# An encoder trunk on one core: large tiles in one common set, B outputs as one run, another opening, grouped norm steps and a last product with the gate inside its weights

## The chip, the cores and the metric

The kernel runs on one core of a Trainium2 chip. The metric is the device time of one execution in microseconds (us); the kernel before has a median of 739.84 us over 3 runs (739.37 to 739.89). A difference of about 0.2% (1.5 us) is the least that such a measurement can tell from no change.

## What is computed

Two layers over x of 256 rows by 1024 columns. Each layer mixes tokens by two attention branches, A (8 query heads on 2 key heads, dense) and B (3 dilated groups of 4 heads, combined by their softmax denominators), gated and summed, and then channels by a squared-ReLU MLP. Both halves have an RMS norm with shift, scale and gate from a vector c.

```python
for l in range(2):
    sh1, sc1, gt1, sh2, sc2, gt2 = split(silu(c) @ w_ada[l] + b_ada[l], 6)
    h = rms(x, g_mix[l]) * (1 + sc1) + sh1
    parts = split(h @ w_in[l])                    # 1024 x 5120: A's q, k, v; B's 3 x (q, k, v); 2 gates
    y_a = attention(rope(rms(qa)), rope(rms(ka)), va) @ w_branch_a[l]
    y_b = dilated(rope(rms(qb)), rope(rms(kb)), vb) @ w_branch_b[l]
    x = x + gt1 * ((sigmoid(ga) * y_a + sigmoid(gb) * y_b) @ w_out[l])
    h2 = rms(x, g_mlp[l]) * (1 + sc2) + sh2
    x = x + gt2 * (square(relu(h2 @ w_ff1[l])) @ w_ff2[l])
```

## The kernel before

**Precision and weights.** Every float32 weight tile of 128 x 1024 (512 KB) is loaded from HBM into one of 7 buffers `wr`; ACT copies it to a rounded high part and DVE subtracts to get the low part (`split_next`). A product then takes three matmuls, high by high, low by high and high by low (`mm3`, `many`). So 512 columns of output cost TensorE (PE) three passes, and each weight tile costs ACT one and DVE one instruction of 1024 columns.

**The vector c.** 96 more tiles of 512 KB (`w_ada`) go through `wr` as well; DVE multiplies each by silu(c) and sums it along the row, in one instruction (`ada_tile`). Their place among the rest is written into the lists `seq0`, `seq1` (letter w), `ada_f0` and `ada_f1`.

**Order of the work.** The program text records operations. A planner (`Plan.issue`) then runs a list scheduler with a cost for each operation, due times, the number of buffers of each kind and pauses for clashes between DVE and GpSimd (POOL), and writes each engine's instructions out in the planned order; the chip keeps that order and waits where the plan was wrong. Letters in `seq0` and `seq1` set the order in which the mixer's parts are recorded: `c` is a chunk of 512 columns of q, k, v, `u` and `v` a half of a gate, `a` and `b` steps of the two attentions, `y` the product with w_branch_a. `OPEN` sets the first loads, the order of the first steps and the engine of each small operation of the opening; `shift` moves due times of single operations.

**Opening.** x comes in two halves, `x0` (with identity, biases and tables, 128 x 1552) and `x1` (128 x 1280); `a0` and `a1` are the first two tiles of w_ada (shift and scale of the first 128 columns of h), `wx` and `wy` the first tiles of w_in (chunks 0 and 1; 2 and 5). `step_x` norms and transposes a half of x, `step_a` makes shift and scale, `step_h` h's first 128 columns, `step_m` its product with wx or wy. One of the two, wy, is used plain in float32, without a split. From then on the loop over k = 1 to 7 does, for each k, two ada tiles, two weight tiles and 24 matmuls.

**Norm of q and k.** `qk_post` takes a chunk's sums from PSUM: ACT copies and squares, DVE sums the squares over each head (`rstd`), adds epsilon, POOL raises to the power -0.5, and DVE combines `t1` (sum by cosine table, read from PSUM) with `t2` (by sine table, POOL's in layer 0, DVE's in layer 1), multiplies by `rstd`, and PE transposes the result.

**Attention.** `att_a_soft` and `att_b_soft` (before: `att_b_pair`) take scores from PSUM, make probabilities `pr`, transpose them on PE, and ACT copies the transposes to SBUF (`keep_pt`, before: buffers of the small kind `s2k`). The products with the values have 64 output columns, two at a time side by side on PE. In B each of two pairs of heads has its own run of 12 such products.

**MLP.** `ff1` makes 512 hidden columns at a time; their squares are split into high and low (`split_hid`, before: `r2k`, 8 small buffers). The last product of layer 1 is cut so that the last output is 256 columns wide; then DVE multiplies by the gate (`gtb`), adds x, and a DMA writes out.

**Buffers.** `b8` is the common set of 8 KB tiles per partition (split weights, hT, tables, attention): 14 before. `s2k` has 7 tiles of 2 KB.

## Time and profile before

| what | value |
|---|---|
| median of 3 runs | 739.84 us |
| the profiled execution | 738.93 us |
| its span, first to last instruction | 737.1 us |
| granted TensorE clock, mean | 0.999 |
| PE busy | 728.7 us (99%) |
| DVE busy | 591.1 us (80%) |
| ACT busy | 469.9 us (64%) |
| POOL busy | 70.2 us (10%) |
| HBM | 178.73 MB read, 244 GB/s over the span |

Matmuls are pipelined, so the busy time of PE is not its work at the peak; what counts is where a matmul starts later than the one before it would allow. In rows of the timeline the columns are start (us from the span's start), length (us), engine, line, operation, what it writes and reads, its form (for PE rows by columns of the array, then the output), count, and in brackets the idle time before it and what ended it. All operations have line 655, at which the planner issues them, so rows are told apart by their tiles: `w` is a split weight, `wr` a raw one, `ps` a PSUM bank, `xin` holds x and the identity, `hT` the transposed and split h, `s2k` any small tile. A float32 matmul (a transpose, or scores) is recorded as more than one.

### The profile page before, as it was taken

The numbers are of one execution on the slowest core, as the hardware profiler recorded it, in microseconds if no ns is written. First come the engines' busy times: TensorE is split into PE (matmuls) and PEld (weight loads), VectorE is DVE, ScalarE is ACT, GpSimd is POOL, SyncE is SP. The second block draws the span as 40 slices with busy tenths as digits, with TensorE's granted clock in tenths as the row PEclk, the third lists the DMA queues.
The fourth block names the chain that finished last, engine by engine and source line by source line (L and its number), as shares of the span: only waits on it lengthen the run. The fifth ranks groups of instructions, "written<-read, shape, count | busy, mean of one in ns | idle before, by whom it ended". The sixth has DMA issues, their size and how long they took to land.

```text
span 737.1 us, 10423 instructions
## 1 busy us (share of the span) xinstructions
PE 728.7 (99%) x3750; PEld 601.1 (82%) x3750; DVE 591.1 (80%) x906; ACT 469.9 (64%) x784; POOL 70.2 (10%) x60
## 2 busy tenths in 40 slices
PE   8999999999999999999999999999999999999998
PEld 5887877788888888888887788877888888888887
DVE  6999999899899989575499977988878975675623
ACT  6569497975758666655366856698537866455530
POOL 0008730000000060000002211000000000000000
PEclk9999999999999999999999999999999999999999
DMA  9997578997499999776256555988546986686201
GB/s 352 409 409 241 158 241 268 337 334 258 144 351 380 392 340 321 260 243 198 70 167 229 183 175 161 369 293 315 193 142 192 371 279 191 223 275 191 77 1 57
DMA packets 50227, 180.47 MB, mean 245 GB/s; under 512 B 5600, under 2 KB 6016, under 8 KB 50176
## 3 DMA queue, kind: packets, MB, share of 16 engines
q1 hardware_dynamic: 50176, 179.82, 69.6%
q8 instruction: 29, 0.48, 0.3%
q14 instruction: 22, 0.18, 0.1%
HBM read 178.73 MB, written 1.06 MB: 244 GB/s over the span
## 4 chain that ended last, share of the span: by engine, by line
PE 94%; DVE 3%; ACT 1%; DMA 1%; POOL 1%; issue 0%; SPq 0%
PE ps L655 94%; DVE s2k L655 1%; DMA wr<-in_w_ada 1%; ACT s2k L655 1%; DVE rstd L655 1%; POOL rstd L655 0%; ACT pr L655 0%; SPq L655 0%; POOL s2k L655 0%; ACT hT L655 0%; DVE w20wx L655 0%; DVE w L655 0%; DVE shg L655 0%; DVE xT L655 0%; DVE tabs L655 0%
## 5 line engine op out<-in xcount | busy, mean ns | idle before, releaser
L655 DVE TENSOR_TENSOR w<-wr,w 128x1024 fp32r<-128x1024 f32 x234 | 284.5, 1238 | 55.6 <-ACT w L655 55.2
L655 ACT ACTIVATE w<-wr 128x1024 fp32r<-128x1024 f32 x234 | 242.3, 1059 | 82.7 <-PE ps L655 56.5
L655 PE MATMUL ps<-w,hT 128*128 128x512 f32 x1032 | 251.1, 396 | 0.1
L655 PEld LDWEIGHTS ps<-w,hT 128*128 128x128 f32 x1032 | 189.7, 188 | 41.9 <-issue 2.2
L655 PE MATMUL ps<-w,r2k 128*128 128x512 f32 (+1 forms) x792 | 178.8, 385 | 0.0
L655 PEld LDWEIGHTS ps<-w,r2k 128*128 128x128 f32 x792 | 144.5, 188 | 30.1
L655 PE MATMUL ps<-hT,w 128*128 128x512 f32 (+1 forms) x896 | 159.7, 338 | 0.0
L655 PEld LDWEIGHTS ps<-hT,w 128*128 128x128 f32 x896 | 138.1, 188 | 20.3
L655 DVE CUSTOM_DVE_ANT_0 s2k<-wr,c_act 128x1024 bf16<-128x1024 f32 x96 | 116.6, 1227 | 3.2 <-DMA wr<-in_w_ada 3.1
L655 ACT ACTIVATE s2k<-ps 128x512 f32<-128x512 f32 (+2 forms) x136 | 61.4, 483 | 77.1 <-PE ps L655 67.0
L655 PE MATMUL ps<-w,mT 128*128 128x512 f32 x192 | 45.6, 393 | 0.0
L655 ACT ACTIVATE s2k<-s2k 128x512 f32<-128x512 f32 (+1 forms) x62 | 38.5, 620 | 6.6 <-DVE s2k L655 5.8
L655 PEld LDWEIGHTS ps<-w,mT 128*128 128x128 f32 x192 | 35.6, 188 | 7.2
L655 POOL TENSOR_TENSOR rstd<-rstd,half 128x8 f32<-128x8 f32 (+1 forms) x20 | 34.5, 1738 | 68.9 <-DVE rstd L655 68.8
L655 ACT ACTIVATE pr<-pr,st 128x256 f32<-128x256 f32 (+1 forms) x64 | 36.1, 611 | 3.0 <-DVE st L655 3.0
L655 DVE TENSOR_TENSOR s2k<-ps,s2k 128x256 f32<-128x256 f32 x56 | 23.4, 420 | 16.8 <-ACT s2k L655 16.7
L655 POOL TENSOR_TENSOR ss<-ss,half 128x1 f32<-128x1 f32 x8 | 4.4, 556 | 296.2 <-DVE ss L655 296.2
L655 DVE TENSOR_TENSOR r2k<-s2k,r2k 128x512 fp32r<-128x512 f32 x28 | 20.1, 719 | 15.5 <-ACT r2k L655 15.2
L655 DVE TENSOR_TENSOR s2k<-ps,gtb 128x512 f32<-128x512 f32 (+1 forms) x18 | 11.8, 660 | 23.6 <-PE ps L655 23.4
L655 PEld LDWEIGHTS ps<-xin,s2k 128*128 128x128 f32 x180 | 21.2, 140 | 7.8 <-ACT pr L655 1.3
L655 PE MATMUL ps<-xin,s2k 128*128 128x128 f32 x180 | 26.4, 275 | 1.1 <-ACT pr L655 0.9
L655 ACT ACTIVATE s2k<-xin 128x512 bf16<-128x512 f32 x14 | 8.7, 623 | 26.4 <-DVE xin L655 26.1
(97 smaller groups left out, 512.0 us busy)
## 6 DMA issues: line engine op xcount, KB each, us to landing
wr<-in_w_ff SPq DMA_DIRECT2D x120, 512.0 KB, 5.0
wr<-in_w_ada SPq DMA_DIRECT2D x96, 512.0 KB, 5.2
wr<-in_w_gate SPq DMA_DIRECT2D x32, 512.0 KB, 4.5
wr<-in_w_qkv SPq DMA_DIRECT2D x24, 512.0 KB, 4.8
wr<-in_w_x SPq DMA_DIRECT2D x16, 512.0 KB, 5.9
wr<-in_w_out SPq DMA_DIRECT2D x16, 512.0 KB, 5.3
wr<-in_w_y SPq DMA_DIRECT2D x8, 512.0 KB, 6.5
wr<-in_w_ba SPq DMA_DIRECT2D x8, 512.0 KB, 6.3
```

Source lines behind the costliest of these rows:

```text
L655: getattr(self.real[o["e"]], o["op"])(*map(real, o["a"]), **{n: real(z) for n, z in o["k"].items()})
```

## The change

- The squares of the hidden columns (`hid`), B's transposed outputs (`ob`) and the attentions' transposed probabilities (`pt_home`) become tiles of the common set `b8`, now of 16; `r2k` and `ob` as kinds of their own are gone, `s2k` grows from 7 to 9.
- B's products with the values, 24 of a layer, are recorded as one run after the second pair's softmax (`att_b_out`).
- The opening loads x0, a0, a1, x1, wy, wx in place of x0, x1, a0, a1, wx, wy, does its steps in another order, and has other engines for seven of its small operations. The mask is loaded after the opening's weights and not before 62 us of the plan (in place of after k = 3).
- In `qk_post`, adding epsilon to `rstd` and the product `t1` are a group: DVE does them one right behind the other.
- At the end of layer 1, of the last 256-column products, those with the last two weight tiles use weights that DVE has multiplied by the gate, rounded and split beforehand (`gated`). They stand behind all others, in banks of their own, so that what is left after the last matmul is one addition.
- The lists `seq0`, `seq1`, `ada_f0`, `ada_f1`, `shift` and some constants of the planner's model (COLD, RATE, SOON, the cost of a copy from PSUM) have new values.

```diff
-  post0=(5, 2, 1, 0), s2k=7, r2k=8, ahead=1, last="k",
+  post0=(5, 2, 1, 0), s2k=9, ahead=1, last="k",
-  seq0="v u c3 w a w c4 v w w u a w b w w u w w w w w a a v w w v w w b w y w y w w w w v y y w w".split(),
-  seq1="w w a w c2 u c3 a u w w c4 v u c5 w w w w b b v v w w w a u w a w y w w w w w y w v y y w w w".split())
+  seq0="a v u c3 a w w w w w c4 v w u w w a w w u b v a w w w v y w w w w w b w w w y w w y y v w".split(),
+  seq1="a a w w a w w c2 u c3 a c5 u w w w w w w u c4 w v w b b v y v u v y w w y w w w w w w w y w w".split())
-NB8 = 14
+NB8 = 16
-    loads="x0 x1 a0 a1 wx wy",
-    steps="C T1 X0 A X1 H0 Wx H1 Mx0 Wy My0 T0 My1 Mx1",
+    loads="x0 a0 a1 x1 wy wx",
+    steps="T1 C Wy A X0 T0 H0 Wx X1 H1 Nx0 Lx0 My0 Mx1 My1",
...
-        dve.tensor_scalar(r, r, HD * EPS, None, op0=ALU.add)
+        with plan.together():
+            dve.tensor_scalar(r, r, HD * EPS, None, op0=ALU.add)
+            dve.tensor_tensor(v4(t1), v4(ps[:, :n]), bc(ct, HD), op=ALU.mult)
         pool.tensor_tensor(r, r, half[:, :nh], op=ALU.pow)
-        dve.tensor_tensor(v4(t1), v4(ps[:, :n]), bc(ct, HD), op=ALU.mult)
...
+    def pt_home(nm):
+        return tl("sbuf", [P, 4, 512], F32, "b8", NB8, f"pT{nm}")
...
         for hp in range(2):
-            att_b_pair(l, T, hp, ops)
+            zs.append(att_b_soft(l, T, hp))
             if hp == 1:
+                ops = pb(f"ob{l}")
+                with plan.together():
+                    for i in range(2):
+                        att_b_out(T, i, zs[i], ops)
                 finish_o(ops, T["ob"], slice(0, 2))
...
         def hid_tiles(j):
-            return [(r2k(f"hh{l}_{j}_{u}"), r2k(f"hl{l}_{j}_{u}")) for u in range(2)]
+            z = tl("sbuf", [P, 2, 2, 512], F32R, "b8", NB8, f"hid{l}_{j}")
+            return [(z[:, u, 0], z[:, u, 1]) for u in range(2)]
...
+        gated = tl("sbuf", [P, 2, 2, 512], F32R, "b8", NB8, "gated")
+        for q, (_, _, w) in enumerate(ws[6:]):
+            wg = s2k(f"wg{q}")
+            dve.tensor_tensor(wg, raw_of[w[0].tile.name][:, 512:1024], gtb[l, 1][:, 512:1024], op=ALU.mult)
+            act.activation(gated[:, q, 0], wg, AF.Copy)
+            dve.tensor_tensor(gated[:, q, 1], wg, f32(gated[:, q, 0]), op=ALU.subtract)
...
+        for c0 in halves:
+            cs = slice(c0, c0 + 256)
+            acc = pb(f"gated{c0}")[:, :256]
+            for q, (j, i, w) in enumerate(ws[6:]):
+                wh, wl = (gated[:, q, z, c0 - 512 : c0 - 256] for z in range(2))
+                mm3(acc, *last_rows(j, i), wh, wl, q == 0, q == 1)
+            dve.tensor_tensor(x[:, 1, cs], x[:, 1, cs], acc, op=ALU.add)
             sp.dma_start(out[1, :, cs], x[:, 1, cs])
```

Three places of the instructions as they stand. First, the loads on SP's queue from the start of the program; before:

```order
L655 DMA c_in<-in_c 128x136
L655 DMA xin<-in_x 128x1552
L655 DMA xin<-in_x 128x1280
L655 DMA wr_83<-in_w_ada 128x1024
L655 DMA wr_84<-in_w_ada 128x1024
L655 DMA wr_85<-in_w_x 128x1024
L655 DMA wr_86<-in_w_y 128x1024
L655 DMA wr_87<-in_w_ada 128x1024
```

and of the change:

```order
L666 DMA c_in<-in_c 128x136
L666 DMA xin<-in_x 128x1552
L666 DMA wr_83<-in_w_ada 128x1024
L666 DMA wr_84<-in_w_ada 128x1024
L666 DMA xin<-in_x 128x1280
L666 DMA wr_85<-in_w_y 128x1024
L666 DMA wr_86<-in_w_x 128x1024
L666 DMA wr_87<-in_w_ada 128x1024
```

The second half of x (128x1280) has moved behind the two w_ada tiles, and wy ahead of wx.

Second, DVE at the norm of chunk 2 in layer 1, its two row blocks (`rstd_128` and `rstd_129` before, `rstd_130` and `rstd_131` after); before:

```order
L655 TENSOR_SCALAR rstd_128<-rstd_128 128x8
L655 TENSOR_REDUCE rstd_129<-s2k_93 128x8
L655 TENSOR_TENSOR s2k_97<-s2k_94,tabs_254 128x8x32
L655 TENSOR_SCALAR rstd_129<-rstd_129 128x8
L655 TENSOR_TENSOR s2k_93<-ps_72,tabs_254 128x512
L655 TENSOR_TENSOR s2k_96<-s2k_96,s2k_97 128x512
L655 TENSOR_TENSOR s2k_94<-s2k_99,tabs_254 128x8x32 x2
L655 TENSOR_TENSOR s2k_96<-s2k_96,rstd_128 128x512
L655 TENSOR_TENSOR s2k_93<-s2k_93,s2k_94 128x512
L655 RECIPROCAL st_144<-st_144 128x2
L655 RECIPROCAL st_145<-st_145 128x2
L655 TENSOR_TENSOR s2k_93<-s2k_93,rstd_129 128x512
```

and of the change:

```order
L666 TENSOR_SCALAR rstd_130<-rstd_130 128x8
L666 TENSOR_TENSOR s2k_97<-ps_73,tabs_260 128x512
L666 TENSOR_SCALAR rstd_131<-rstd_131 128x8
L666 TENSOR_TENSOR s2k_93<-ps_76,tabs_260 128x512
L666 TENSOR_TENSOR oa_274<-ps_74,oa_274 128x2x256
L666 TENSOR_REDUCE st_138<-ps_79 128x2
L666 TENSOR_REDUCE st_139<-ps_72 128x2
L666 TENSOR_TENSOR s2k_100<-s2k_98,tabs_260 128x8x32 x2
L666 TENSOR_TENSOR s2k_95<-s2k_96,tabs_260 128x8x32
L666 RECIPROCAL st_138<-st_138 128x2
```

Behind each epsilon there is now an operation that reads PSUM (`ps`), five of them before the next one with both inputs in SBUF; before, most of what follows has both inputs in SBUF (`s2k`, `tabs`, `rstd`).

Third, PE where B's products with the values stand in layer 1 (`v_267`, `v_273` are the values); before, from the start of the second of two runs of this form, 18 rows behind the end of the first:

```order
L655 MATMUL ps_74<-w_307,hT_264 128x512 x4
L655 MATMUL ps_76<-s2k_94,v_267 64x256
L655 MATMUL ps_76<-s2k_99,v_267 64x256
L655 MATMUL ps_76<-s2k_94,v_267 64x256
L655 MATMUL ps_76<-s2k_99,v_267 64x256
L655 MATMUL ps_76<-s2k_97,v_267 64x128
L655 MATMUL ps_76<-s2k_95,v_267 64x128
```

and of the change:

```order
L666 MATMUL ps_73<-w_319,hT_270 128x512 x4
L666 MATMUL ps_76<-pTb_0_313,v_273 64x256 x4
L666 MATMUL ps_76<-pTb_0_313,v_273 64x128 x8
L666 MATMUL ps_76<-pTb_1_314,v_273 64x256 x4
L666 MATMUL ps_76<-pTb_1_314,v_273 64x128 x8
L666 MATMUL ps_73<-w_319,hT_270 128x512 x2
```

Both pairs' 12 products stand together, with matmuls over all 128 output rows only ahead and behind.

132 lines of the change are left out of this document (72 added, 60 removed).

## The prediction

> **What bounds the kernel now.** First the page: which engine is busy, and which one the chain of work that ended last runs through.
>
> ```profile
> PE 728.7 (99%) x3750; PEld 601.1 (82%) x3750; DVE 591.1 (80%) x906; ACT 469.9 (64%) x784; POOL 70.2 (10%) x60
> ...
> PE 94%; DVE 3%; ACT 1%; DMA 1%; POOL 1%; issue 0%; SPq 0%
> ```
>
> PE has 99% and 94% of the chain. PE's instructions are the same 3567 before and after, in other groups; so the time can change only where PE starts, where it waits or loses time between matmuls, and behind its last matmul. The chain in order of time shows these places.
>
> ```profile
> 18.08 36.96 PE ps L655 x160
> ...
> 64.12 133.59 PE ps L655 x735
> ...
> 419.58 138.75 PE ps L655 x742
> ...
> 733.59 0.44 DVE s2k L655
> 734.03 0.02 issue
> 734.05 0.42 DVE xin L655
> ```
>
> The reader sees long stretches of PE, a start of 18 us ahead of them, breaks in which the chain runs through other engines (the one that ends at 64.12 and the one that ends at 419.58 are priced below), and 0.9 us of DVE behind the last matmul. A break in the chain is not all PE idleness: PE often has other work. The page's own count of idle PE is 737.1 - 728.7 = 8.4 us, most of it at the start and the end. That is all there is to win by waiting less, and what follows sorts it.
>
> **The opening.** Timeline of DVE and PE, the load of x1, and two stretches of the windows (busy us of PE, PEld, DVE, ACT, POOL; clock; DMA share; GB/s).
>
> ```profile
> 7.13 0.15 DVE L655 SCALAR_TENSOR_TENSOR ss<-ss 128x1 f32<-128x1 f32 x1
> ...
> 8.67 1.22 DVE L655 CUSTOM_DVE_ANT_0 s2k<-wr,c_act 128x1024 bf16<-128x1024 f32 x1 [0.30 <-DMA wr<-in_w_ada]
> ...
> 9.96 1.23 DVE L655 CUSTOM_DVE_ANT_0 s2k<-wr,c_act 128x1024 bf16<-128x1024 f32 x1
> ...
> 11.42 0.68 DVE L655 COPY xT<-ps 128x512 f32<-128x512 f32 x1
> 12.02 0.34 DVE L655 TENSOR_SCALAR s2k<-xT,shg 128x128 f32<-128x128 f32 x1
> ```
> ```profile
> xin<-in_x SPq DMA_DIRECT2D x1, 640.0 KB, 5.7
> ```
> ```profile
> 19.00:58.00 39.00, 39.00 (x172) 31.70 (x171) 37.51 (x63) 24.17 (x32) 1.48 (x2) 1.00 1.03 408
> 58.00:93.00 35.00, 34.74 (x166) 28.16 (x164) 33.76 (x51) 24.04 (x43) 28.02 (x22) 1.00 0.59 186
> 93.00:153.00 60.00, 60.00 (x388) 47.11 (x388) 55.82 (x107) 53.62 (x119) 6.79 (x6) 1.00 0.83 285
> ```
> ```profile
> 12.63 1.10 PE L655 MATMUL ps<-wr,s2k 128*128 128x512 f32 x2 [1.36 <-DVE hT L655]
> ...
> 19.36 0.91 PE L655 MATMUL ps<-w,hT 128*128 128x512 f32 x3
> ```
> ```profile
> 24.38 0.43 DVE L655 TENSOR_TENSOR hT<-s2k,hT 128x256 fp32r<-128x256 f32 x1
> ```
>
> DVE waited 0.30 us for a0 at 8.67, and took a1 as soon as it had landed. x1 is now behind them: its 655 kB at 408 GB/s are 1.6 us, so both land 1.6 us earlier, near 7.05 and 8.35. DVE is free at 7.28: two products of 1.2 us bring it to 9.65 in place of 11.19; the copy of xT (0.6 until the next can start), two small steps (0.45) and h's first columns (0.34) end near 11.05 in place of 12.36. wy now has the place of wx, which ACT was able to take at about 11.2 to 11.4, so the first plain product starts there in place of 12.63: 1.2 to 1.4 us earlier. That is the upper end.
>
> Not all of it lasts. The loop over k that starts at 19.36 takes two ada tiles and two splits of DVE per k, and x1 is later, so its norms are too (DVE has two of them now, 0.48 each, and has given a copy, a cast and a sum of squares to ACT). The second ada tile for k = 2 is the 13th load in both kernels: 6.76 MB at 408 GB/s, counted on from x1's landing (1.66 + 5.7 = 7.4 us at 1.52 MB), land near 20.2. From there, in the new order: that product to 21.5, the split of k = 1's second tile to 22.65, shift and scale to 22.95, ACT's two steps of 0.6 to 24.15. PE begins k = 2 there; before it began at 19.36 + 24 x 0.23 = 24.9, which its inputs (24.38) had not held up. So **0.7 us** stay, between 0 (DVE's and the loads' pace decide) and 1.4. From k = 3 on DVE needs about 5.3 us per k against PE's 5.5, and the mask's 256 KB (0.64 us) are out of the way, so nothing is lost again.
>
> **The breaks.** PE's waits, with what POOL and DVE did there.
>
> ```profile
> 64.12 0.63 PE L655 MATMUL ps<-xin,s2k 128*128 128x128 f32 x4 [0.26 <-DVE rstd L655]
> ```
> ```profile
> 413.22 5.48 POOL L655 TENSOR_TENSOR rstd<-rstd,half 128x8 f32<-128x8 f32 x2 [12.27 <-DVE rstd L655]
> ```
> ```profile
> 414.65 0.68 DVE L655 TENSOR_TENSOR s2k<-s2k,s2k 128x512 f32<-128x512 f32 x1
> ```
> ```profile
> 418.74 0.69 DVE L655 TENSOR_TENSOR s2k<-s2k,rstd 128x512 f32<-128x512 f32 x1 [1.39 <-POOL rstd L655]
> ```
> ```profile
> 419.58 0.63 PE L655 MATMUL ps<-xin,s2k 128*128 128x128 f32 x4 [0.88 <-ACT pr L655]
> ```
> ```profile
> 75.67 3.29 POOL L655 TENSOR_TENSOR rstd<-rstd,half 128x8 f32<-128x8 f32 x2 [0.74 <-DVE rstd L655]
> ```
> ```profile
> 76.18 1.28 DVE L655 TENSOR_TENSOR s2k<-s2k,s2k 128x512 f32<-128x512 f32 x2
> ```
>
> Two powers on POOL took 3.29 us at 75.67 (1.64 each) and 5.48 us at 413.22: 2.2 us more, while DVE went through operations with both inputs in SBUF without a pause (from 414.65 on). DVE then waited 1.39 us for the second power, and PE 0.88 us for transposes of the same norm, though the releaser named there is ACT, which ended at the same time. In the new order five operations that read PSUM stand behind the first epsilon, some 3 us, in which both powers find room. I take the **0.88 us** (0 if ACT's softmax was the true cause) and the **0.26 us** at 64.12, which fall to the earlier start of the first norm and the group (0 if not).
>
> By the Trainium skill (SBUF — State Buffer, section "Who interferes with whom") a DVE operation with two SBUF inputs and a POOL operation that reads SBUF exclude each other, and the one issued first holds the other off to its end. The 5.48 us agree with the half in which POOL waits. The other half would speak against the group, since POOL would now come first; what that would cost is a rival below. At 76.18 two such DVE operations took their usual 0.64 us each inside a power, which does not agree.
>
> **B outputs as one run.** Rows around one run (24 records are its 12 products), with the usual pace of a matmul of 512 columns.
>
> ```profile
> L655 PE MATMUL ps<-w,r2k 128*128 128x512 f32 x744 | 173.1, 392 | 0.0
> ```
> ```profile
> 149.86 0.87 PE L655 MATMUL ps<-w,hT 128*128 128x512 f32 x3
> 150.66 1.96 PE L655 MATMUL ps<-s2k,v 128*64 128x256 f32 x24
> ```
> ```profile
> 152.55 0.96 PE L655 MATMUL ps<-w,hT 128*128 128x512 f32 x3
> ```
>
> A matmul of 512 columns takes 173.1 / 744 = 0.233 us of PE. The three ahead of the run take 0.80 to its start, 0.1 more than 0.70; the three behind it are 0.96 long against 2 x 0.233 + 0.39 = 0.86, again 0.1 more. Inside the run the rows don't part the change of the array's shape from the work; I take 0.1 (0 to 0.2). That is 0.3 for each run, and two of them (one per layer) go: **0.6 us**, between 0.4 and 0.8. What the run now waits for, the second pair's softmax, holds nothing up: B's result is first read by the product with w_bb at the mixer's end.
>
> **The end.** Behind the last matmul stood a product by the gate (0.44, with 0.02 of issue) and an addition (0.42). The product goes: **0.46 us**. The addition of the 256-column sum, now with one PSUM input, keeps its length as the product with one PSUM input had the same 0.42 to 0.44. The added work, two gate products, two high and two low parts, is about 3 us of DVE and ACT that falls before PE needs it: DVE is idle for most of the last 15 us, and the last split is done some 4 us before its use.
>
> Tiles in `b8` or `s2k`, the moved ada tiles, and the moved mask cost nothing by count: no instruction gets longer. Their cover is the stock of split weights; if a tile comes free late, PE waits for a split.
>
> **The sum.** 0.7 + 0.88 + 0.26 + 0.6 + 0.46 = 2.9 us off the profiled execution (738.93), which stands 0.9 below the median of 739.84. Off the median: **736.9 us**. The bounds add up to 0.9 and 3.8, that is 736.0 to 739.0; new waits may add some tenths to it.
>
> **Rivals.**
> - *DVE paces layer 0.* DVE was 96% busy in 19 to 58 and 58 to 93, and 93% in 93 to 153. If PE's earlier start meets DVE at its limit, what was won until 153 us is waited away; left are the end (0.46) and layer 1's run (0.3): 739.1. For it: those shares. Against it: 6.9 us of idle DVE in these stretches, against 1.3 to be made up. Chance 0.17.
> - *Powers held off in new places.* The norm of chunk 3 in layer 1 has, behind the second pair of epsilon and t1, seven operations in a row with both inputs in SBUF; the second power falls into them. One that is held off as at 413 costs 2.2 us, if PE's transposes have no slack. Two at full price would give 736.9 + 4.5 = 741.4, slower than before; from the second one on this decides. For it: the row of 5.48. Against it: the mean of 1.93 us over 16 such powers, so that only a few were held off at all. Chance 0.09.
> - *POOL first holds DVE.* A power that begins beside t1 runs about 1.0 us past it. If it held DVE for that time at 20 norms, layer 0's 10 would cost more than the 5.4 idle us of DVE from 58 to 153, some 3.5 us of PE: 740.4. This is the page's rule; the row at 76.18 speaks against it. Chance 0.04.
> - *The opening keeps all.* If the loads of k = 2 land earlier than I count, 1.4 us stay: 736.2. Chance 0.05; it lies inside the range.
>
> **How the numbers follow.** The forecast has 0.65, the full opening 0.05: faster by over 0.2% (below 738.4) has 0.70. DVE's pace and POOL first are within 0.2%, 0.21. Held-off powers are slower, 0.09. About 0.2%, 1.5 us, is what a measurement of this kernel can tell from no change. The range takes the forecast with its bounds and DVE's pace and leaves out the two others: 735.4 to 739.4.
>
> **What would show it.** Right: the first plain product on PE at 11.2 to 11.4 us, k = 2 near 24.2; no PE wait over 0.3 us near 61 and in 380 to 420; powers of at most 2 us behind chunk 2 of layer 1; one run of 48 records per layer; a single DVE operation behind the last matmul, near 731. Wrong: PE idle between 19 and 153 us beyond some tenths with DVE named (DVE's pace), powers over 3 us with PE waiting for the transposes behind them, or DVE operations of 1.5 us beside a power.

## The result and the profile after

The changed kernel takes 739.83 us (median of 12 executions, 738.53 to 741.65) against 739.64 of the kernel before in the same comparison (12, 739.25 to 740.20): a ratio of 1.0004, interval 0.9997 to 1.0011. **No change**, where 736.9 was forecast, and above the range's end of 739.4. The profiled execution took 738.55 us (span 736.8); before it was 738.93 (span 737.1).

The page of the changed kernel, busy time and the engines of the chain that ended last:

```profile
PE 730.5 (99%) x3750; PEld 601.3 (82%) x3750; DVE 590.5 (80%) x910; ACT 471.8 (64%) x788; POOL 67.4 (9%) x60
...
PE 91%; DVE 5%; issue 1%; DMA 1%; ACT 1%; POOL 0%; DVEq 0%
```

PE is the bound as before. Its idle time fell from 8.4 to 736.8 - 730.5 = 6.3 us, yet the span only by 0.3: the same 3750 records count 1.8 us more of busy time (the 16 products of c alone are one row of 2.88 us before and of 3.78 after). So idle time by itself does not measure the gain. The chain in order of time (start, length, what) tells where the gain stopped:

```profile
11.73 7.34 PE ps L666 x28
19.09 6.51 DMA wr<-in_w_ada
...
30.82 24.66 PE ps L666 x105
...
56.13 0.70 DVE rstd L666
...
88.44 0.69 DVE st L666
89.15 2.33 ACT pr L666 x9
...
91.53 6.79 PE ps L666 x41
...
107.67 626.00 PE ps L666 x3260
733.70 0.42 DVE xin L666
```

The breaks at 64.12 and 419.58 are gone: from 107.67 on the chain is one stretch of PE. Ahead of it the chain leaves PE in three places where it had stayed on PE before: for a w_ada load (6.51 us, to 25.60), for a long stretch that is mostly DVE's, from 56.13 on, and ends in a softmax on ACT before 91.53, and for ACT and DVE before 107.67.

To place the difference, both kernels are compared at points of equal work: the first matmul of k = 3, the last of k = 7, the first product of the mixer's output in each layer, the last matmul, the last DVE instruction. The mixer's output products (`w,mT`), before and then after:

```profile
169.35 0.63 PE L655 MATMUL ps<-w,mT 128*128 128x512 f32 x2
...
530.01 0.63 PE L655 MATMUL ps<-w,mT 128*128 128x512 f32 x2
```
```profile
170.83 0.63 PE L666 MATMUL ps<-w,mT 128*128 128x512 f32 x2
...
529.88 0.63 PE L666 MATMUL ps<-w,mT 128*128 128x512 f32 x2
```

| stretch | before us | after us | difference | forecast |
|---|---|---|---|---|
| start to k = 3 on PE | 30.34 | 30.82 | +0.48 | -0.7 |
| k = 3 to the end of k = 7 | 27.46 | 27.88 | +0.42 | 0 |
| to mixer output, layer 0 | 111.55 | 112.13 | +0.58 | -0.56 |
| to mixer output, layer 1 | 360.66 | 359.05 | -1.61 | -1.18 |
| to the last matmul's end | 203.54 | 203.78 | +0.24 | 0 |
| behind the last matmul | 0.93 | 0.46 | -0.47 | -0.46 |
| sum | | | -0.36 | -2.9 |

Layer 1 did what was forecast, and a little more; everything until 170 us went the other way. The other profiles of both kernels show which rows repeat. The second and third do: two more profiles of the kernel before (`e15_before_1`, `e16_before_2`, below) have 27.5 and 111.5 us there, and the changed kernel's repetition has 27.9 and 112.2. Three others do so less. The start to k = 3 is 30.54 in the undisturbed one of those two and 30.65 in the repetition, so that this row can be as small as +0.1. Layer 1's row is -1.4 by these profiles. And the stretch to the last matmul is 203.91 in both further profiles of the kernel before, so that its +0.24 is no loss by the change.

Of the 1.28 us between the median (739.83) and the profile (738.55), 0.8 come from executions in which the clock granted to PE fell in the opening, the last group of experiments: without them the median is 739.04. The rest is that the profiled execution is a fast one; the same holds before (738.93 against 739.64).

### The profile page after: what moved, and what is told of

The parts are those of the page before. It is cut to its first block, busy times and chain, and to the rows that moved or that the text cites. A ratio compares the mean times of both kernels' runs of the same rounds, so it can differ in the third digit from the quotient of the medians.

```text
span 736.8 us, 10385 instructions
## 1 busy us (share of the span) xinstructions
PE 730.5 (99%) x3750; PEld 601.3 (82%) x3750; DVE 590.5 (80%) x910; ACT 471.8 (64%) x788; POOL 67.4 (9%) x60
## 4 chain that ended last, share of the span: by engine, by line
PE 91%; DVE 5%; issue 1%; DMA 1%; ACT 1%; POOL 0%; DVEq 0%
PE ps L666 91%; DVE s2k L666 2%; DVE w L666 2%; DVE rstd L666 1%; DMA wr<-in_w_ada 1%; ACT pr L666 0%; POOL s2k L666 0%; ACT s2k L666 0%; ACT w L666 0%; DVE shg L666 0%; DVE st L666 0%; ACT c_act L666 0%; DVE xT L666 0%; ACT pTa L666 0%; DVE xin L666 0%
## 5 line engine op out<-in xcount | busy, mean ns | idle before, releaser
L666 PE MATMUL ps<-w,hid 128*128 128x512 f32 (+1 forms) x780 | 176.4, 385 | 0.0
L666 PEld LDWEIGHTS ps<-w,hid 128*128 128x128 f32 x780 | 143.0, 188 | 29.2
L666 ACT ACTIVATE s2k<-ps 128x256 f32<-128x256 f32 (+3 forms) x104 | 43.8, 446 | 74.2 <-PE ps L666 73.4
L666 DVE TENSOR_TENSOR hid<-s2k,hid 128x512 fp32r<-128x512 f32 x28 | 19.7, 703 | 25.4 <-ACT hid L666 25.2
L666 POOL TENSOR_TENSOR rstd<-rstd,half 128x8 f32<-128x8 f32 (+1 forms) x20 | 30.7, 1542 | 86.5 <-DVE rstd L666 85.9
L666 POOL TENSOR_TENSOR s2k<-s2k,tabs 128x256 f32<-128x256 f32 (+1 forms) x20 | 19.8, 1004 | 60.3 <-ACT s2k L666 48.8
```

The source lines that it names most:

```text
L666: getattr(self.real[o["e"]], o["op"])(*map(real, o["a"]), **{n: real(z) for n, z in o["k"].items()})
```

## Experiments

Most edits change the time that the plan gives to single operations before each engine's order is written out. Only the place of these operations in their engine's order changes; buffers and all else stay. In the diffs, cut to the lines that matter, the numbers are those of operations in the program text: `MOVED` names operations and the one right ahead of which they go (`late` is -0.01; the first three edits write the same as pairs). The medians of these kernels differ also by how often the clock fell in the opening (the last group), so the first groups are read from points of equal work in the profiles.

```diff
+        at = list(start)
+        for ops, j, late in MOVED:
+            for i in ops:
+                at[i] = at[j] + late
-        order = self.order = sorted(self.ops, key=lambda o: (start[o["i"]], rank[o["e"]], o["i"]))
+        order = self.order = sorted(self.ops, key=lambda o: (at[o["i"]], rank[o["e"]], o["i"]))
```

### What sets k = 3 in the opening

The theory: PE starts k = 3 a fixed chain behind the w_ada tiles for k = 3, so an earlier start of PE can't last. The rivals: the order of DVE's steps, PE's own pace, or the place of the mask's load.

**The changed kernel again**, without an edit, in five rounds.

> The changed kernel, unchanged, a second time. Its 12 times lie between 738.53 and 741.65, where those of the kernel before lie between 739.25 and 740.20. If the loads of the opening pace it (theory L), the scatter sits there: a second profile shows another landing of k = 3's ada tiles than 25.60 us, and k = 3 on PE (30.82 in the first profile) and the first key transposes (62.34) move with it. If DVE's pace in layer 0 makes the loss (theory D), the opening repeats within 0.2 us, and 1.5 us more than before stand again at the start of layer 0's w_out product (170.83 against 169.35 before). Time: 739.8, from 738.5 to 741.7.

738.65 against 739.29, ratio 0.9997 (0.9988 to 1.0005): again no change.

**The mask before k = 3's first w_ada tile**, as it stood before.

```diff
+MOVED = [(375, 180)]
```

> The changed kernel with one instruction moved: the load of the mask (256 KB) is issued ahead of k = 3's first ada tile again, at about 18 us; all else keeps its order and its buffers. Theory L (the loads pace k = 3): every tile behind it lands 0.64 us later (256 KB at 404 GB/s), k = 3's ada tiles at 26.2 and 27.5, k = 3 on PE at 31.4 in place of 30.8, and the kernel takes 0.4 to 0.7 us longer, about 740.4. Theory D (DVE's order and work pace it): DVE waits 0.6 longer ahead of the ada products, but makes it up by 107 us, and the time stays within 0.2 us.

739.94, ratio 1.0015 (1.0003 to 1.0027). k = 3 moved by 0.1 us only in the profile, to 30.91. But the first part of the tile that it hangs on landed at 25.14 in place of 24.51, and these 0.63 us are what 256 KB take at 406 GB/s; only the last part came at nearly the same time (26.98 against 26.88), because the parts lay closer together here.

**A split first.** The low part of k = 2's second tile on DVE stands before k = 3's first w_ada product, which waited 1.15 us for its load.

```diff
+MOVED = [(167, 181)]
```

> The changed kernel with one instruction moved: on DVE the low part of k = 2's second weight tile (it ran at 28.16) goes ahead of the two ada products of k = 3, for which DVE stood idle 1.15 us from 24.58. Theory L: the second ada tile lands at 26.9 and sets the start of its product, the low part fits into the wait, so DVE reaches k = 3's shift and scale at 28.3 in place of 29.3; PE's waits at 28.74 (0.31) and 30.24 (0.18) go, k = 3 starts at 29.9 to 30.0, 0.8 us earlier; by 58 us 0.5 to 0.9 are left, and 739.0 to 739.3 if nothing takes them back. Theory D: the same in the opening, but PE's gain is waited away between 62 and 108 us, where DVE has under 0.6 us idle: w_out's product still starts near 170.8 and the time stays at 739.8.

740.25, ratio 1.0015 (1.0007 to 1.0024).

**wy's last plain product four matmuls earlier** on PE, which gives its raw buffer back sooner.

```diff
+MOVED = [(101, 96)]
```

> The changed kernel with one instruction moved: on PE the last plain product with the raw w_y tile (it began at 18.04) goes ahead of four products with w_x's halves, so the raw tile is free about 0.9 us earlier and SP, which waited for it until 19.09 (1.3 us of waiting for PE), issues k = 3's first ada tile at about 18.2. Theory S (the slot held by that tile delays the loads): k = 3's ada tiles land 0.9 us earlier, near 24.7 and 26.0, k = 3 on PE at 29.9 and 0.5 to 0.9 us off the time: 739.0 to 739.3. Theory L (the queue is full at 404 GB/s, and a tile lands when the bytes ahead of it are through): landings stay at 25.6 and 26.9 within 0.1, k = 3 stays at 30.8 and the time at 739.8.

739.36, ratio 1.0008 (0.9997 to 1.0019).

None of the three won anything: among the executions at a clock of 0.999 or more the medians are 738.62 for the changed kernel as it is, 739.35 with the mask early, 739.38 with the split first and 738.83 with wy's product earlier.

DVE and PE around k = 3, first in the changed kernel:

```profile
25.73 1.23 DVE L666 CUSTOM_DVE_ANT_0 s2k<-wr,c_act 128x1024 bf16<-128x1024 f32 x1 [1.15 <-DMA wr<-in_w_ada]
...
27.01 1.23 DVE L666 CUSTOM_DVE_ANT_0 s2k<-wr,c_act 128x1024 bf16<-128x1024 f32 x1
...
28.16 1.22 DVE L666 TENSOR_TENSOR w<-wr,w 128x1024 fp32r<-128x1024 f32 x1
```
```profile
18.49 10.63 PE L666 MATMUL ps<-w,hT 128*128 128x512 f32 x44
...
30.82 1.42 PE L666 MATMUL ps<-w,hT 128*128 128x512 f32 x4 [0.18 <-ACT hT L666]
```

Then with wy's product earlier, and with the split first:

```profile
25.20 1.22 DVE L670 CUSTOM_DVE_ANT_0 s2k<-wr,c_act 128x1024 bf16<-128x1024 f32 x1
...
26.98 1.23 DVE L670 CUSTOM_DVE_ANT_0 s2k<-wr,c_act 128x1024 bf16<-128x1024 f32 x1 [0.55 <-DMA wr<-in_w_ada]
```
```profile
30.79 2.57 PE L670 MATMUL ps<-w,hT 128*128 128x512 f32 x9 [0.16 <-ACT hT L670]
```
```profile
25.88 1.23 DVE L670 TENSOR_TENSOR w<-wr,w 128x1024 fp32r<-128x1024 f32 x1 [0.52 <-ACT w L670]
27.02 1.22 DVE L670 CUSTOM_DVE_ANT_0 s2k<-wr,c_act 128x1024 bf16<-128x1024 f32 x1
```

k = 1 began on PE at 18.49 us (before 19.36), but k = 3 at 30.82. The chain from the second w_ada product to PE is 30.82 - 27.01 = 3.81 us: the product, a split, two small steps, ACT's two steps. It is 30.79 - 26.98 = 3.81 with wy's product earlier, although there the first tile landed 1.1 us earlier and only the second was waited for. Counted from the landing of the second tile by the DMA records, k = 3 follows 3.93 to 3.96 us later in these five profiles; in those, k = 1 began anywhere from 18.49 to 19.37. With the split first, the split itself waited 0.52 us for ACT's high part, the products came 1.1 to 1.3 us later, and k = 3 stayed at 30.95.

The kernel of `e8_cover` (below), whose edit lies far behind, has the same opening, and there the second tile landed at 26.13:

```profile
26.27 1.23 DVE L671 CUSTOM_DVE_ANT_0 s2k<-wr,c_act 128x1024 bf16<-128x1024 f32 x1 [0.39 <-DMA wr<-in_w_ada]
```

k = 3 began 3.94 us behind that landing, at 30.07, and the span is 736.1 us in place of 736.8. So **the landing of k = 3's tiles sets k = 3**, 3.9 us before it, and it differs from execution to execution (26.13 to 26.99 in these six). PE's pace is not the cause. Of DVE's order only one other was tried, and that split had to wait for ACT.

Before the change, the tile landed at 26.63 and PE reached k = 3 at 30.34 by its own pace; the loads had been just fast enough. An earlier PE had little to gain there. In both kernels the tile was later than its bytes: by the count of the prediction, carried on by 4 tiles of 1.28 us, it would land at 25.4 after the change, and it landed at 26.88. The DMA engines were full, as the traffic between 4 and 30 us shows:

```profile
DMA packets 2836, 10.55 MB, mean 406 GB/s; under 512 B 318, under 2 KB 318, under 8 KB 2835
```

A tile comes in 16 parts. In the changed kernel's profile the first and the last part of one landed 0.9 us apart up to 23 us, and 2.4 for k = 3's tiles; for the second of these it is 1.6 before the change, and 1.6 to 2.4 in the six profiles above. So what the later mask saves was lost on the last part: the first part of that tile landed 0.49 us earlier than before the change, the last 0.25 us later. A 16 KB instruction fetch of about 1 us stands at that place, before the change too (at 22.97 us). That it parts them was not tried.

**The opening before in the changed kernel**, and **the new opening alone in the kernel before** (with the planner's new costs):

```diff
-    loads="x0 a0 a1 x1 wy wx",
+    loads="x0 x1 a0 a1 wx wy",
...
-    shift={143: -3327, 206: 5401})
-COLD = 5200.0
+    shift={})
+COLD = 9000.0
```

> The changed kernel with the opening of before (order of loads and steps, engines, both plain products with w_y, mask at k = 3); the planner orders the rest anew, so what lies behind 60 us is not the same order. Theory C (the clock): in the changed kernel, and in three kernels with its opening, 21 of 58 executions had a granted clock of 0.995 to 0.998 and took 1.5 to 4 us longer, and of 47 executions of the kernel before not one; if the new opening brings this, no execution here is below 0.999, the 12 times lie within 2 us, and the median falls to that of the undisturbed ones, 738.0 to 738.6. Theory R (something behind the opening brings it: the long run of B outputs, the waits at 90 and 107 us): a third of the executions is low here too, and the median stays at 739.5. Both: k = 3 on PE at 30.3 as before.

739.88, ratio 1.0006 (0.9997 to 1.0014).

```diff
-SOON = 200.0
+SOON = 150.0
...
-    loads="x0 x1 a0 a1 wx wy",
+    loads="x0 a0 a1 x1 wy wx",
...
-COLD = 9000.0
+COLD = 5200.0
```

> The kernel before with the new opening alone (loads, steps, engines, one plain product per row tile, late mask, and the planner's numbers for them); all behind it is of before, ordered anew by the planner. Theory C: a third of the executions shows a clock under 0.999, k = 3 on PE starts at 30.7 to 30.9 (the second ada tile lands at 26.7 to 27.0, and 3.94 us later PE starts, in all five profiles), 0.4 later than before, so the median is 0.5 to 1.5 us above that of before: 739.9 to 740.8. My forecast's opening term: 0.7 us faster, 738.6. Theory R: the clock stays at 0.999 and above, the median at 739.7 to 739.9.

742.2, ratio 1.0039 (1.0027 to 1.0052), 5 executions: slower, where the forecast's term would have made it faster.

Neither isolates the opening, since the planner ordered more than the opening anew: in the first, k = 3 came at 32.47, 6.0 us behind its tile (26.47); in the second at 31.81, and it has a wait of PE of 0.88 us at 202.42 that neither kernel has there (its 0.89 at 422.65 is the break of the kernel before). The rest can still be read: from k = 3 to the end of the span are 737.1 - 30.34 = 706.8 us before, 736.8 - 30.82 = 706.0 after, and 738.1 - 32.47 = 705.6 with the opening before. All parts of the change but the opening are worth 0.8 to 1.2 us together by these, not the 2.2 of the forecast.

### Layer 0: two new waits

```profile
91.53 0.33 PE L666 MATMUL ps<-xin,pr 128*128 128x128 f32 x1 [0.62 <-ACT pr L666]
...
107.67 0.55 PE L666 MATMUL ps<-xin,s2k 128*128 128x128 f32 x3 [0.22 <-DVE s2k L666]
```

In the new order A's scores stand at 86.22 (93.00 before), and PE comes to the transposes of their probabilities before ACT is done; later it comes to a norm's transposes too early for DVE. Together 0.84 us, in place of 0.26. The theory: DVE's pace; the rival: the chain of one softmax on ACT, with too little work of PE placed in front of it. What speaks for DVE at the first wait: in the chain of the changed kernel DVE's work leads, but for one piece of POOL's (2.15 us), from 56.13 to the maxima at 88.44, with which the softmax can begin, and DVE is busy for 98% of the time around it:

```profile
58.00:93.00 35.00, 34.38 (x171) 27.71 (x170) 34.47 (x58) 24.36 (x52) 25.27 (x23) 1.00 0.60 191
```

**More cover.** Ten PE operations that stood behind the transposes are put ahead of them.

```diff
+MOVED = [(range(727, 737), 480, -0.01)]
```

> The changed kernel with ten PE products moved: those that use a weight tile already split (w_qkv's tile ready at 88.5 us) all stand ahead of the first transposes of A's softmax, for which PE waited 0.61 us at 91.5. Theory O (the fixed order of PE makes this wait): the wait goes, nothing takes its place, w_out and w_mix start 0.6 us earlier counted from k = 3's start, and the time falls by 0.6. Theory D (the softmax and the splits are as late as ACT and DVE make them; ACT is busy without a pause from 89.1 to 98 us): PE comes 0.6 us or more too early to the next pair's transposes (95.4) and waits there, w_mix starts where it did within 0.1 us, and the time stays.

740.23, ratio 1.0009 (0.9999 to 1.002).

**More cover, and less of DVE:** the same, and six w_ada products between read half of their columns. This kernel leaves out half of six sums, so its results are not those of the others.

```diff
+HALF = [683, 685, 687, 689, 691, 813]
...
+                if o["i"] in HALF:
+                    a[:3] = [z[:, :512] for z in a[:3]]
```

> The kernel of e8 (ten products ahead of A's softmax transposes) with six ada products on DVE between 80 and 108 us cut to half their columns, which leaves out half of the sum for six tiles and takes 3.7 us off DVE there. Theory D (DVE's pace is what moved PE's wait from 91.5 to 94 and 106 us in e8): PE's waits between 85 and 110 us (0.5 in e8) go, and w_mix of layer 0 starts 139.4 to 139.6 us behind k = 3's start in place of 140.0 to 140.1. Rival (ACT's softmax, busy without a pause from 89 to 98 us, is the pace): waits for it of 0.3 us stay near 94 and the distance stays at 139.9 to 140.1.

739.64, ratio 0.9998 (0.9988 to 1.0007).

What PE waited for around these places (us, times, longest), with more cover, then with less of DVE's work as well:

```profile
PE ps L671 <- ACT pr L671: 0.2, 1, 0.2
PE ps L671 <- DVE s2k L671: 0.2, 1, 0.2
```
```profile
PE ps L675 <- ACT pr L675: 0.2, 1, 0.2
PE ps L675 <- DVE s2k L675: 0.2, 1, 0.2
```

The cover cut ACT's wait from 0.62 to 0.23, at 94.42 us. What is left does not change when DVE has 3.3 us less to do (six products of 0.68 us in place of 1.23), so **DVE's pace is not the cause of these two remaining waits**.

For the 0.62 of the changed kernel the run speaks the other way: the two products that were halved ahead of the softmax took 1.1 us off DVE, and the softmax began 57.29 us behind k = 3, against 58.33 in the changed kernel and with the cover alone, while A's scores stood at the same place. So DVE set when the softmax began, and without the cover PE came to it too early; less DVE work without the cover was not tried.

Ahead of the 0.22 stand three DVE operations of 0.70, 1.75 and 1.22 us (from 101.77, 104.72 and 106.39) whose like take 0.17, 1.22 and 0.69 elsewhere, each of them beside an operation of POOL with `tabs`; they are as long with less DVE work (0.69, 1.75, 1.23). That POOL makes this wait was not tried.

From k = 3 to the mixer's output it is 140.07 us with the cover and 139.88 with less DVE work, against 140.01 in the changed kernel: what was saved at the wait was lost elsewhere in the stretch, and I did not find where. The waits are not the changed kernel's in every order: in the run with the opening before, which has the whole ordered anew, A's scores stand later behind the loop, PE has no wait of 0.15 us or more between the loop and the mixer's output, and from the end of k = 7 to the mixer's output it needs 110.84 us, against 111.55 before the change and 112.13 after it.

### What a run of B's products costs

**Two runs** in each layer again, the second pair's 12 products behind further products over the whole array (about 3 us of them), in the changed kernel's buffers.

```diff
+MOVED = [(range(1155, 1167), 1239, -0.01), ((1167,), 1239, 0.01), ((1168,), 1239, 1300.0), (range(3745, 3757), 3832, -0.01), ((3757,), 3832, 0.01), ((3758,), 3832, 1300.0)]
```

> The changed kernel with one thing moved in each layer: on PE the second pair's 12 B products stand behind 14 further products of w_out and the gate (layer 1: behind the same stretch), so each layer has two runs of 24 records in place of one of 48 (the two readers of the result follow). My price: 0.3 us for each run, 0.6 in all. If it holds, w_mix's first product (170.83) moves 0.3 us further from k = 3's start, the one of layer 1 (529.88) 0.6, and the median is 0.6 up. Rival: a change of shape hides behind the weight loads and the move costs under 0.1 us in each layer.

741.02, ratio 1.0021 (1.0009 to 1.0034). In layer 0 the runs stand at 154.97 and 159.85 us. The stretch from the end of k = 7 to the mixer's output is 112.61 us, against 112.13 to 112.22 in ten profiles with one run; from there to layer 1's, 359.73 against 359.05 to 359.32. A run costs **0.4 to 0.5 us** in layer 0 and 0.4 to 0.7 in layer 1, where the rows beside it gave 0.3.

Then layer 0 should have won 0.4, and did not. The kernel before shows why:

```profile
123.62 1.96 PE L655 MATMUL ps<-s2k,v 128*64 128x256 f32 x24
125.51 2.00 PE L655 MATMUL ps<-ka,qk 64*128 64x256 f32 x16
```

There, one of the two runs stood right against A's scores, another form with half of the array, so that the array went back to its whole form once for both. I count stretches of such forms between whole ones, and leave out a single product of 8 columns, `ps<-xin,gcol`: 7 in layer 0 before and 7 after; 7 in layer 1 before and 5 after (A's products and scores now touch at 417 as well):

```profile
415.27 1.95 PE L666 MATMUL ps<-pTa,v 128*64 128x256 f32 x16
417.14 2.00 PE L666 MATMUL ps<-ka,qk 64*128 64x256 f32 x16
```

With 0.4 to 0.5 for each, layer 1 saves 0.8 to 1.0, and with the wait of 0.88 some 1.7 to 1.9; 1.61 was measured, and 1.3 to 1.65 with the other profiles of both kernels. Layer 0 saves none, and its waits grew by 0.84 - 0.26 = 0.58; 0.58 was measured. The count is open, though. With the product of 8 columns it is 8 and 8 in layer 0, and 8 before and 7 after in layer 1, where that product touched another stretch before and stands alone after; layer 1 would then save 0.88 + 0.4 to 0.5 = 1.3 to 1.4, which fits the other profiles better. The price of a run is shown; that a stretch of another form has the same price, and which ones count, is argued.

### What held POOL's power at 413 us

After the change both powers there take their usual 1.6 us:

```profile
417.09 3.24 POOL L666 TENSOR_TENSOR rstd<-rstd,half 128x8 f32<-128x8 f32 x2 [14.07 <-DVE rstd L666]
```

3.24 us for two, where before it was 5.48, and PE's wait of 0.88 is gone. The long one hangs on the order: the second power took 3.88 us in all three profiles of the kernel before and in its version with the new opening, and never over 1.65 at this place in those of the changed kernel whose order there is unedited. Whether DVE's train of operations with both inputs in SBUF was the cause can be tried.

**The train behind the second epsilon:** five DVE operations with both inputs in SBUF are moved ahead of four that read PSUM (the second t1, A's output and the softmax's maxima).

```diff
+MOVED = [((3187, 3188, 3202, 3203, 3193), 3206, -0.01)]
```

> The changed kernel with DVE's order behind chunk 2 of layer 1 turned back towards that of before: five operations with both inputs in SBUF (four of 128x256, one of 128x512, 2.3 us) go from behind the PSUM readers to right behind the second epsilon (417.7). My step (a train of two-input SBUF operations holds the power on POOL): one of the two powers, 1.64 us each now, takes 3.5 to 4.0 us, DVE waits for it ahead of the last product of that norm, and PE waits up to 0.9 us for the transposes (424.2); layer 1's w_mix, 359.05 to 359.31 us behind layer 0's in the undisturbed profiles, comes 0.4 to 0.9 later. Rival (the 3.88 us of before had another cause): both powers stay below 1.9 us and the distance stays within 0.15 of 359.2.

741.1, ratio 1.003 (1.0017 to 1.0043). DVE, POOL and PE in this kernel:

```profile
421.29 0.75 DVE L671 TENSOR_TENSOR s2k<-s2k,tabs 128x256 f32<-128x256 f32 x2
422.07 0.69 DVE L671 TENSOR_TENSOR s2k<-s2k,s2k 128x512 f32<-128x512 f32 x1
422.68 0.76 DVE L671 TENSOR_TENSOR s2k<-s2k,tabs 128x256 f32<-128x256 f32 x2
```
```profile
420.79 3.47 POOL L671 TENSOR_TENSOR rstd<-rstd,half 128x8 f32<-128x8 f32 x2 [14.07 <-DVE rstd L671]
```
```profile
427.65 0.33 PE L671 MATMUL ps<-xin,pr 128*128 128x128 f32 x1 [1.68 <-ACT pr L671]
```

DVE went through 2.1 us of such operations inside the two powers; these took 3.47 us (1.64, and 1.87 for the second), and DVE's operations their usual time. So the explanation of the 5.48 us is **not confirmed**, and stays open. The test is weaker than the case before: about 1.0 us of the train lay inside the second power here and 2.3 there, and the train there also had products that read `rstd`. The time was lost elsewhere: the maxima came later, so ACT's softmax did, and PE waited 1.68 us. It shows what those PSUM reads at this place are worth: they let the softmax begin.

### The granted clock in the opening

The executions of the changed kernel lie in two groups, some 2 us apart, and those of the kernel before nearly all in one. The upper group has a mean granted clock of 0.995 to 0.998. In the changed kernel the 8 executions at 1.0 have a median of 739.04 us, the 4 at 0.998 one of 741.40, and in its repetition it is 738.62 and 740.77: a fall goes with 2.1 to 2.4 us more here (1.4 to 3.3 in its edited versions). Below 0.999 were 45 of 105 executions in the ten runs with the new opening as it is, none of 11 in the changed kernel with the opening before, and 1 of 118 of the kernel before beside them.

Windows of 3.4 us (busy us of PE, PEld, DVE, ACT, POOL; granted clock; DMA share; GB/s) in an execution with a fall, of the kernel with two runs in each layer, and PE there:

```profile
4.60:8.00 3.40, 1.34 (x12) 1.15 (x11) 1.55 (x7) 1.80 (x4) 0.00 (x0) 1.00 1.02 384
8.00:11.40 3.40, 3.09 (x13) 1.95 (x14) 2.32 (x5) 1.79 (x4) 1.47 (x1) 0.50 1.01 410
```
```profile
8.02 1.44 PE L671 MATMUL ps<-s2k,xin 64*128 64x128 f32 x6 [2.07 <-DVE s2k L671]
```

PE was idle for 2.07 us before the transposes of x0, and busy for 1.34 of 3.40 us; then the clock was 0.50 for a window, and the transposes ran at half pace. The theory: a stretch of about 3.4 us with PE busy for less than half of it lowers the clock for the next; here PE has done c's matmuls and waits for x0. The rival: chance, with no link to PE's idleness. Short matmuls in the gap tell them apart.

**Five small matmuls in the gap**, repeats of the warming product behind the last matmul of c.

```diff
+                if o["i"] == 33:
+                    z = self.ops[3]
+                    for _ in range(5):
+                        self.real["PE"].matmul(*map(real, z["a"]), **{n: real(q) for n, q in z["k"].items()})
```

> The changed kernel with five more of the idle products with the constant tile on PE, behind the sixteen of c (1.1 us at full clock), into a bank that nothing uses then. In the profile of e7 PE stood idle from 5.94 to 8.02 us, its clock fell to half at 8.03 for 3.41 us, and k = 1 and k = 3 came 1.5 and 0.7 us late. Theory I (idle PE in this stretch drops the clock): no execution below 0.999, the times between 738.0 and 739.5, median 738.4 to 738.9, below that of the kernel before. If the clock falls for another reason, 4 or 5 of 11 are below 0.999 as in the other kernels with this opening, and the median is 739 to 740.

738.97, ratio 0.9995 (0.9986 to 1.0003); 1 of 11 below 0.999.

**x1's load first**, ahead of a0 and a1, as before.

```diff
+MOVED = [((11,), 9, -0.01)]
```

> The changed kernel with one instruction moved on SP: x1 is loaded ahead of the two ada tiles again, as before. Theory Q (the order of loads delays x0, which in e6 and e7 landed at 6.5 and 6.4 in place of 5.6 to 6.0, and so makes PE idle): no execution below 0.999. Theory P (the new order of steps leaves PE less work there: 8 table products in place of 16 behind the first diagonal): a third or more of the executions stays below 0.999. Either way the ada products start 1.3 us later (a0 lands at 8.6), k = 1 on PE at 19.8 to 20.3 and k = 3 at 31.0 to 31.5, so about 0.4 us are lost; median 739 to 740.

738.58, ratio 0.9995 (0.9986 to 1.0005); 2 of 12 below 0.999.

**x1 first, and the table products of x's second half** moved on PE ahead of x0's transposes, right behind those of the first:

```diff
+MOVED = [((11,), 9, -0.01), ((17, 18, 19, 20), 45, -0.01)]
```

> The kernel of e11 (x1 loaded ahead of the ada tiles) with the four products of the second row tile's tables, which then have their data, moved on PE to behind the first four, ahead of x0's transposes: 16 table products in a row, as before. Theory P (PE has too little work behind the first tables): no execution below 0.999, where e11 had 2 of 12. Theory X (the clock falls because x0 lands late, at 6.4 us and more in all four profiles with a fallen clock, before any table product can run): 2 to 4 of 12 stay below 0.999. k = 1 and k = 3 as in e11's undisturbed runs within 0.3 us, median 738.4 to 739.

740.06, ratio 1.0008 (0.9999 to 1.0017); 8 of 11 below 0.999, more than in any other. PE in it:

```profile
12.98 1.27 PE L671 MATMUL ps<-wr,s2k 128*128 128x512 f32 x2 [2.31 <-DVE s2k L671]
```

The products were now missing ahead of the first plain product: another gap, of 2.31 us, with x0 landing at 6.05 us, not late.

**x1 first with the five small matmuls:**

> The kernel of e11 with e10's five idle products behind those of c: both changes that cut the low-clock executions (2 of 12 and 1 of 11, against 45 of 105 in the ten kernels with the new opening as it is). Theory I (PE idle while x0 is on its way drops the clock; 1.1 us of idle products lift the share of work): none or one of 12 below 0.999, median 738.3 to 738.9, faster than the kernel before by 0.05 to 0.15%. If the clock hangs on something else: 2 or more of 12, median 738.6 to 739.5.

739.16, ratio 0.9994 (0.9985 to 1.0003); none of 11 below 0.999. PE is busy for 2.69 us of the first window now, and no gap there is over 0.71 us (a later one, at 12.85, is 1.38):

```profile
4.60:8.00 3.40, 2.69 (x26) 2.50 (x27) 1.58 (x6) 1.80 (x4) 0.39 (x1) 1.00 1.01 397
```
```profile
5.53 1.28 PE L675 MATMUL ps<-warm 128*128 128x128 f32 x10
7.52 1.14 PE L671 MATMUL ps<-s2k,xin 64*128 64x128 f32 x8 [0.71 <-DVE s2k L671]
```

**The kernel before, two more profiles**, one execution each, for x0's landing and the clock.

> The kernel before once more, for its profile: in its 97 other executions the clock was below 0.999 once. Theory X: x0 lands before 6.0 us (5.68 in the first profile), since nothing else would spare it. Theory P: x0 lands late here in a third of the executions too (6.4 and more), with the clock at 1.0 all the same.

> As e15, a third profile of the kernel before. The first matmul behind the loop's start (k = 3) at 30.3 to 30.4 as PE's own pace gives it, 0.7 us or less behind what the landing of the second ada tile (26.63 in the first profile) and 3.94 us would allow: the loads don't pace it.

739.61 with x0 landing at 5.92 and the clock at 1.0; and 740.47 with x0 at 6.28 and a fall:

```profile
4.60:8.00 3.40, 1.48 (x14) 1.29 (x15) 1.67 (x7) 1.90 (x5) 0.03 (x1) 1.00 0.99 393
8.00:11.40 3.40, 3.40 (x16) 1.80 (x16) 3.01 (x7) 2.98 (x6) 1.53 (x2) 0.51 1.03 423
```
```profile
7.87 1.95 PE L655 MATMUL ps<-s2k,xin 64*128 64x128 f32 x8 [1.92 <-DVE s2k L655]
```

So the kernel before falls too when x0 lands late; it does so rarely. In the 18 profiles of this study I laid periods of 3.41 us from the point where the clock first rises (4.1 to 7.4 us). After each of the six periods of the opening at full clock in which PE was busy for a share of 0.32 to 0.44, the next was at half clock; after those with 0.50 or more it never was. Where the periods lie differs from execution to execution: in the kernel before with the new opening x0 landed at 6.52 us, late, but the gap was shared by two periods (0.55 and 0.66 busy), and the clock stayed. The matmuls in the gap took away nearly all falls. **The link to PE's idle share is shown**: by the periods, by the gap that was moved and brought 8 falls in 11, and by the matmuls, since 1 fall in 22 executions with them is not what chance makes of 45 in 105 (11 of the 22 had x1 first as well; that alone had 2 falls in 12).

Why x0 lands late more often in the new opening (6.28 to 6.84 us in five of the falls, 5.6 to 6.1 in most other profiles) is open: it is the second load in both, but a0 and a1 follow it now. Its first part lands at 4.7 to 5.1 us in all 18 profiles; only the last part differs, 0.8 to 2.0 us behind the first, and the next ten tiles keep nearly the same distance (0.9 us in the changed kernel's profile, 1.5 in that of two runs).

The two versions with the small matmuls are the best found, at 0.05% under the kernel before; both intervals reach beyond 1, so they can't be told from no change either.

## Why the prediction was wrong

- **The opening, -0.7: wrong, +0.48 by k = 3** in this pair of profiles, +0.1 by another. The first part held in the main: the first plain product came at 11.73 (forecast 11.2 to 11.4; before 12.63), since DVE's first w_ada product waited 0.63 us for silu(c) on ACT, and k = 2 at 24.37 (forecast 24.15 to 24.2), 0.5 earlier. The step that failed is "From k = 3 on DVE needs about 5.3 us per k against PE's 5.5, and the mask's 256 KB (0.64 us) are out of the way, so nothing is lost again". Loads were followed to k = 2 and then only DVE's pace was compared. k = 3's tiles land at 26.9, and the chain of 3.9 us behind them gives 30.8, later than PE's old 30.34. That it is later is in part bad luck, as it hangs on how far the tile's parts lie apart: at 26.13, the best seen, k = 3 is 0.3 us earlier than before (0.5 by the other profile), still not 0.7 earlier. The loop has no room after that: PE's weight loads waited three times for hT (0.27, 0.31, 0.27 us) against two before (0.37, 0.20), 0.28 of the +0.42 to k = 7. The weight loads, before and after:

```profile
52.21 0.76 PEld L655 LDWEIGHTS ps<-w,hT 128*128 128x128 f32 x4 [0.37 <-ACT hT L655]
53.16 0.98 PEld L655 LDWEIGHTS ps<-w,hT 128*128 128x128 f32 x5 [0.20 <-DVE hT L655]
```

```profile
31.27 4.84 PEld L666 LDWEIGHTS ps<-w,hT 128*128 128x128 f32 x22 [0.27 <-DVE hT L666]
...
42.77 4.87 PEld L666 LDWEIGHTS ps<-w,hT 128*128 128x128 f32 x22 [0.31 <-DVE hT L666]
47.91 0.19 PEld L666 LDWEIGHTS ps<-w,hT 128*128 128x128 f32 x1 [0.27 <-DVE hT L666]
```

- **The break at 419, -0.88: right in size**, but the reason given for it (the train of SBUF operations holds the power) is not confirmed. The rule of the Trainium skill (SBUF — State Buffer, section "Who interferes with whom") speaks for a hold in one direction or the other there; in the row at 420.79 DVE's operations kept their time, and the second power took 0.23 us more than the first. POOL's longer operations agree with it: beside those that read `tabs` or write them, DVE operations of 1.22 us took up to 2.04 in both kernels.
- **The break at 64, -0.26: gone, but replaced** by 0.62 at 91.53 and 0.22 at 107.67. "New waits may add some tenths" was right in kind; it was taken off no number, and it was 0.84.
- **Two runs fewer, -0.6:** the price was too small (0.4 to 0.5, not 0.3) and the count too large. One of the removed returns of the array in layer 0 was already shared with A's scores, so that no stretch went there; layer 1 lost one or two, by how one counts. The forecast counted runs, not what stands beside them.
- **The end, -0.46: right** (0.93 to 0.46 us behind the last matmul).
- **The rivals.** "DVE paces layer 0" (739.1) comes nearest to the executions without a fall (739.04), and part of its mechanism is there: DVE set when A's softmax began, and so PE's new wait of 0.62. It is not the whole of it, since with more cover the remaining waits did not move with DVE's work, and k = 3 was lost to a load. In the changed kernel no power took over 1.87 us. DVE operations are lengthened there beside POOL's operations with `tabs`, by up to 0.8 us as in the kernel before, but not by a power.
- **Not thought of: the clock.** The row of the windows with the clock was read from 19 us on, where it is 1.00. Ahead of that PE waits for x0, near the edge at which the clock falls; the new opening goes over it in 4 executions of 10. Without them the changed kernel would stand 0.6 us under the one before (739.04 against 739.64), with them 0.2 over it. The Trainium skill (TensorE: Matmul & The Clock Gate, section "Part 1: The HAM clock gate (the "warmup" mystery)") describes a window of about 3.4 us that runs by itself; the periods in these traces, 3.41 us, agree. Its section "HAM oscillation — how this bites in real kernels" gives as the rule no idle gaps above about 3.4 us; here 1.9 to 2.3 us of idle time within one period were enough, in two of the six cases as two gaps.

The terms that failed add up: +1.18 at k = 3, +0.42 to k = 7, +1.14 in layer 0, +0.24 in layer 1's second half, which the other profiles of the kernel before do not repeat, -0.43 in layer 1. With -0.01 at the end that is the 2.54 us between the forecast (-2.9) and what the profile shows (-0.36). (The 3567 instructions of PE in the forecast stand in no page of the profile, which counts 3750 in both kernels; no term hangs on this number.)

## What to carry to other kernels

An earlier start is worth only what the first loop behind it can take: follow the loads, with the engine chain behind each, until the engine that bounds runs on stock again, not to the first iteration that improves. Before counting on fewer changes of the array's form, look at what stands beside each run. And where an opening leaves TensorE idle for about 2 us, look at several executions and their clock; some small matmuls in the gap are cheap insurance.

## What was not expected of the hardware

- The granted clock of TensorE falls to half for a period of 3.41 us, at times two, after a period of the opening with PE busy for 0.44 of it or less; 0.50 kept it. In the changed kernel the executions with a fall took 2.1 to 2.4 us longer.
- A saturated queue (406 GB/s) does not land its tiles in even steps: parts of one 512 KB tile were 0.9 to 2.4 us apart in one profile, and a tile landed 1.5 us later than its bytes. A last part that was late once stayed late for the tiles behind it.
- Two powers on POOL took 3.47 us beside 2.1 us of DVE operations with both inputs in SBUF, and 5.48 us beside others, in every profile with that order; what tells these apart is open.
